# A hybrid encoder layer (axial attention beside a bidirectional mLSTM, then SwiGLU): the opening with squares summed on TensorE and four projection tiles in the first batch

## The chip, the cores and the metric

The kernel runs on one core of a Trainium2 chip. A core has five engines that work side by side, each through its own list of instructions in order: TensorE (PE in the profile; PEld is its weight load) multiplies matrices into PSUM, VectorE (DVE), ScalarE (ACT) and GpSimd (POOL) work on rows of elements, SyncE (SP) issues most transfers. The metric is the device time of one execution, in microseconds (us), the median of several runs.

## The reference

One layer over a sequence of 1024 positions with 1024 features, batch 1, all in float32:

```python
cond = jax.nn.silu(c)
mod = cond @ w_ada[l] + b_ada[l]
sh1, sc1, g1, sh2, sc2, g2 = jnp.split(mod, 6, axis=-1)
h = modulate(rms_norm(x, norm_mix_g[l]), sh1, sc1)      # h*(1+scale) + shift
proj = h @ w_in[l]
q_a, k_a, v_a, qk_m, v_m, o_m, gates = jnp.split(proj, splits, axis=-1)
y_attn = axial_gqa_attention(q_a, k_a, v_a, q_norm_g[l], k_norm_g[l], tables)
y_mem = bidirectional_mlstm(qk_m, v_m, o_m, gates, conv_w[l], conv_b[l], gate_b[l], mlstm_norm_g[l])
mix = jnp.concatenate([y_attn, y_mem], axis=-1) @ w_out[l]
x = x + g1[:, None, :] * mix
h = modulate(rms_norm(x, norm_ffn_g[l]), sh2, sc2)
x = x + g2[:, None, :] * ((jax.nn.silu(h @ w_gate[l]) * (h @ w_up[l])) @ w_down[l])
return rms_norm(x, final_norm_g)
```

The attention has 8 query heads and 2 key heads of 64 features, with a norm and a rotation of q and k; the mLSTM has 4 heads of 128 and runs over chunks of 64 positions in both directions.

## The kernel before

Everything is held transposed: features on the 128 partitions, the 1024 positions along the row. x comes as eight tiles of 128 features (k = 0 to 7); a row is worked on in two halves of 512 positions (n = 0, 1).

**Products in three parts.** A float32 factor is split into a high part, rounded to the fast format fp32r, and the low rest. A product of w and h is then three matmuls into the same sum (`mm3`, L295 to L297): whi x hh, whi x hl, wlo x hh. So each h (tile k, half n) needs ScalarE for `hh` (a copy) and an element-wise engine for `hl` (x - hh: VectorE for k = 0, POOL for the others), and each weight piece ScalarE for `whi` and POOL for `wlo`. A piece is 128 x 512: four k of one tile of 128 output features. Pieces sit in a ring of six; `load_piece` asks for the next one, and its transfer goes through `wst`, a ring of three. In the trace the matmuls of the first batch appear as `acc<-hh,whi`, `acc<-hl,whi`, `acc<-hh,wlo`; those that produce positions on the partitions (for v, o and the gates of the mLSTM) as `acct`.

**The opening.** ScalarE squares each half of a tile of x (`sq<-x`), VectorE and POOL add the squares up (`ssx<-ssx,sq`), and one matmul with ones per half sums over the partitions (`ms<-ssx,ones`, L549). `rstd_steps` makes 1/sqrt from it: a ScalarE estimate, then one Newton step on VectorE (the `sq<-ms`, `sq<-sq` rows). Warm-up matmuls (`acc<-con,ones`) run before and after these sums (WARM0, L547, and WARM, L555); their results are overwritten.

**Modulation.** The row c comes replicated over the partitions as `cond`. For each 128 features of the shift (j = 0 to 7) and of the scale (j = 8 to 15) `ada_load(j)` loads 128 x 1024 weights and multiplies them by `cond` with a running sum (`ada<-ada,cond` on VectorE; j = 0 has its product on POOL and its sum on ScalarE). `h_steps(k)` then adds the biases in columns of 128x1 (`mod<-modacc,vec`), forms the factor (`sc<-mod,vec`), multiplies the tile by rstd on VectorE (`x<-x,sq`), applies factor and shift on ScalarE (`x<-x,mod,sc`), and splits the result.

**The first batch.** For k = 0 to 7 TensorE adds up three projection tiles in PSUM: attention's k, v and q0 (`acc0[0]` to `acc0[2]`). Behind it a stream of units, in the order of `IN`, does the rest of the projection; K and q are rotated by `rope_steps`, v is turned by `v_steps`. At the same time `gate_steps`, a chain of short operations on VectorE and ScalarE with small transposes on TensorE (T, from L819 to L918), prepares the mLSTM's gates. The attention starts with its first score matmul (S, L974) when q's rotation and the gates are done; the rest of the projection fills TensorE's gaps in it. Then comes the mLSTM (`ni<-Cs,mq` is one of its matmuls), with the output projection as filler, then the feed-forward part.

**What sets the order.** The program is written out by a planner, the class `Clock`. Each step is emitted with an expected duration; steps that are ready run in the order of expected times, and `need` holds TensorE's next instruction back until what it needs has been emitted. So the order of each engine's list follows from the costs in the code, such as `ck.pe(0.65)` for three matmuls. Such a list is then fixed: an engine that waits for one instruction lets none of the later ones past.

Of the kernel before, what the change touches and what calls it, by code (L numbers as in the profile page):

```python
# [11 lines left out]
F32 = mybir.dt.float32  # L12
# [28 lines left out]
WARM = 6  # L41
WARM0 = 9
POOLED = (0,)
# [4 lines left out]
IN = ([("t", 0), ("q", 1), ("q", 2), ("q", 3), ("f", 0), ("f", 4), ("f", 1), ("f", 5), ("t", 2), ("f", 2), ("f", 6),  # L48
# [21 lines left out]
class Flag:  # L70
    """done: what sets it is emitted; t: when that is expected to end"""
# [12 lines left out]
class Engine:  # L84
    """An engine's instructions with their expected times."""
# [39 lines left out]
class Clock:  # L125
    """Emits instructions in the order of expected times (us), each engine's in the order in which they are ready."""
# [16 lines left out]
    def chain(self, delay, *steps, flag=None, bg=None):  # L143
        """Functions that follow one another. bg: the engine of each step; the step waits until that is idle."""
# [35 lines left out]
    def need(self, *flags):  # L180
        """What sets the flags is emitted before what follows."""
# [14 lines left out]
    def add_pe(self, dt):  # L196
        """work of the tensor engine that is not a stream's"""
        self.t += dt
# [6 lines left out]
    def streams(self, mains, fills=(), stop=None):  # L205
        """Runs streams, the first that is ready first, until the mains have ended or stop() holds."""
# [14 lines left out]
class Stream:  # L221
    """A part of the tensor engine's work: a generator that yields the flags that its next piece needs."""
# [15 lines left out]
def layer_kernel(ctx, tc, xT, c, w_ada, vecs, cons, rope, w_f, w_t0, w_t, w_o, w_gu, w_d, out):  # L238
# [8 lines left out]
    # ---------------------------------------------------------------- constants  # L247
    both = const.tile([P, 2], F32, name="both")
# [22 lines left out]
    # DRAM scratch  # L271
# [39 lines left out]
    def psum_open(name, tags, bufs=1):  # L311
        """tags: name -> (tag, buffers)"""
# [7 lines left out]
    class slot:  # L320
        """what frees the next tile of a tag"""
# [26 lines left out]
    with tc.manual_schedule():  # L348
# [12 lines left out]
        def load_cond(pool):  # L361
            """silu of c, the same for all partitions"""
# [11 lines left out]
        # ---------------------------------------------------- weights in a ring of six pieces  # L374
# [33 lines left out]
        specs = conv_w(0) + conv_w(1) + conv_w(2)  # L408
# [12 lines left out]
        def raw(shape, src, flag, arrived):  # L421
            """a transfer into the ring of three; flag: it has been used; arrived(tile, delay)"""
# [10 lines left out]
        def split(p, delay, src, shape, *before, lo=None):  # L433
            """the parts of a piece"""
# [12 lines left out]
        def piece(i):  # L447
            """a piece; its transfer, where it has one of its own"""
# [11 lines left out]
        def load_piece():  # L460
            """the next piece, once there is room for it"""
# [17 lines left out]
        # ---------------------------------------------------- norm 1, modulation, first three tiles  # L479
# [11 lines left out]
        ssx = [stp.tile([P, HALF], F32, tag="ssx", name="ssx", bufs=2) for _ in range(NH)]  # L491
        sq_ok = {}
        for k in range(KT):
            def sum_up(k=k):
# [1566 lines left out]
```

## Time and profile before

| | us |
|---|---|
| median of 3 runs (1430.2 to 1435.06) | 1433.75 |
| span of the profiled execution | 1431.8 |
| TensorE busy in it | 1310.1 |
| VectorE busy | 1075.9 |
| POOL busy | 792.6 |
| ScalarE busy | 660.6 |
| TensorE's first instruction (warm-up) | 7.59 |
| first batch done, first `acct` matmul | 89.76 |
| first score of the attention | 206.75 |

A time-line row gives start, duration, engine, line, operation, out<-in, shapes and count, and in brackets how long the engine had been idle and what released it. A row of groups gives line, engine, operation, names and shapes, count, then busy time and the mean in ns, then the idle time ahead. L96 is a helper through which all operations of VectorE, ScalarE and POOL pass, so these are told apart by their names.

### The profile page before, as it was taken

Reading aid. Unit: us, or ns where it says so; the run is one execution under the profiler, and the core shown is the slowest. Engines: PE = TensorE matmul, PEld = TensorE weight load, DVE = VectorE, ACT = ScalarE, POOL = GpSimd, SP = SyncE. Lnnn points to the kernel's source line nnn. Section 1 sums busy time; section 2 is a strip of 40 time slices with the busy share of each in tenths; the row PEclk is TensorE's granted clock in tenths of the full one; section 3 lists DMA queues with packets and bytes.
Section 4 is the critical chain, followed back from the end, with each engine's and each line's share of the span. In section 5 each row is a group of like instructions: output and inputs, shape, how many; then the busy total and the mean of one; then the engine's idle time right before and its main releaser. Section 6 shows DMA issues by size and latency. Waiting matters only on the chain.

```text
span 1431.8 us, 19550 instructions
## 1 busy us (share of the span) xinstructions
PE 1310.1 (91%) x6594; PEld 1075.7 (75%) x6602; DVE 1075.9 (75%) x1542; ACT 660.6 (46%) x1191; POOL 792.6 (55%) x624
## 2 busy tenths in 40 slices
PE   5789799999999999899877899999999999979997
PEld 2577677888878988777655688888888887757786
DVE  6947989987788836776899786766666654988676
ACT  5444326677666645454555333332333234433462
POOL 5555454444444336766557564554544444799942
PEclk9899899999999999999999999999999999999999
DMA  7446452322112144824742342232333159623324
GB/s 285 158 127 198 148 153 78 118 66 77 44 52 60 38 136 127 291 94 165 239 155 67 102 141 103 96 106 101 111 110 102 62 185 339 247 67 88 103 63 151
DMA packets 103172, 184.40 MB, mean 129 GB/s; under 512 B 11296, under 2 KB 32672, under 8 KB 103072
## 3 DMA queue, kind: packets, MB, share of 16 engines
q1 hardware_dynamic: 89968, 161.06, 35.2%
q10 hardware_dynamic: 13104, 22.10, 4.2%
q8 instruction: 52, 0.85, 0.3%
q14 instruction: 48, 0.39, 0.1%
HBM read 136.19 MB, written 43.25 MB: 125 GB/s over the span
## 4 chain that ended last, share of the span: by engine, by line
PE 55%; DVE 19%; issue 8%; DMA 7%; POOL 6%; ACT 3%; SPq 1%; DVEq 0%; POOLq 0%; ACTq 0%
PE acc L296 13%; PE acc L295 13%; PE acc L297 13%; POOL wlo L96 3%; DVE x L96 3%; DVE ada L96 3%; DVE sst L96 3%; PE av L1025 2%; DMA wst<-act_d 2%; PE T L1006 2%; DVE PT L96 2%; PE S L974 2%; DVE y L96 2%; PE acct L295 2%; PE acct L297 1%
## 5 line engine op out<-in xcount | busy, mean ns | idle before, releaser
L96 POOL TENSOR_TENSOR wlo<-wst,whi 128x512 fp32r<-128x512 f32 (+2 forms) x208 | 309.0, 1492 | 227.4 <-ACT whi L96 211.2
L96 ACT ACTIVATE whi<-wst 128x512 fp32r<-128x512 f32 (+2 forms) x219 | 131.9, 606 | 141.8 <-PE acc L297 22.4
L96 POOL TENSOR_SCALAR P<-P,sst 128x1024 f32<-128x1024 f32 x64 | 88.9, 1392 | 141.2 <-DVE sst L96 99.8
L296 PE MATMUL acc<-x,whi 128*128 128x512 f32 x352 | 139.6, 397 | 3.3 <-DVE x L96 3.3
L96 POOL TENSOR_TENSOR wlo<-wr,whi 128x512 fp32r<-128x512 f32 x60 | 83.5, 1392 | 78.3 <-ACT whi L96 74.9
L295 PE MATMUL acc<-hh,whi 128*128 128x512 f32 x224 | 97.8, 436 | 13.5 <-ACT hh L96 11.3
L297 PE MATMUL acc<-whi,wcl 128*128 128x512 f32 x244 | 98.1, 402 | 9.5 <-POOL wcl L96 9.5
L96 ACT ACTIVATE P<-S,sst,colq 128x1024 f32<-128x1024 f32 x64 | 77.3, 1207 | 52.2 <-DVE sst L96 47.8
L295 PE MATMUL acc<-whi,wch 128*128 128x512 f32 x244 | 96.8, 397 | 4.0 <-ACT wch L96 4.0
L296 PE MATMUL acc<-hl,whi 128*128 128x512 f32 x224 | 92.8, 414 | 8.2 <-POOL hl L96 4.5
L296 PE MATMUL acc<-wlo,wch 128*128 128x512 f32 x244 | 96.9, 397 | 1.1 <-POOL wlo L96 1.1
L297 PE MATMUL acc<-hh,wlo 128*128 128x512 f32 x224 | 91.5, 409 | 0.0
L96 DVE SCALAR_TENSOR_TENSOR ada<-ada,cond 128x512 f32<-128x512 f32 (+1 forms) x79 | 84.9, 1082 | 7.3 <-DMA ada<-in_w_ada_dram 7.2
L96 DVE TENSOR_TENSOR sg<-acc,sg 128x512 f32<-128x512 f32 x67 | 45.4, 687 | 59.3 <-PE acc L297 58.9
L96 ACT ACTIVATE PT<-T 128x512 fp32r<-128x512 f32 x128 | 71.4, 597 | 37.8 <-PE T L1006 37.1
L96 DVE TENSOR_TENSOR PT<-T,PT 128x512 fp32r<-128x512 f32 x128 | 82.8, 681 | 7.2 <-ACT PT L96 7.1
L96 ACT ACTIVATE whi<-wr 128x512 fp32r<-128x512 f32 x60 | 37.9, 632 | 106.1 <-DVE wr L96 49.6
L96 POOL TENSOR_TENSOR wlo<-s,whi 128x512 fp32r<-128x512 f32 x44 | 60.8, 1383 | 38.3 <-ACT whi L96 31.7
L295 PE MATMUL acct<-whi,hh 128*128 128x256 f32 (+1 forms) x256 | 79.3, 310 | 2.4 <-ACT xp L96 1.0
L296 PEld LDWEIGHTS acc<-x,whi 128*128 128x128 f32 x352 | 66.5, 189 | 19.2 <-DVE x L96 4.2
L96 DVE SCALAR_TENSOR_TENSOR x<-acc,mod,x 128x512 f32<-128x512 f32 (+1 forms) x92 | 62.7, 719 | 24.1 <-PE acc L297 24.1
L1006 PE MATMUL T<-con,P 128*128 128x128 f32 x512 | 70.2, 275 | 10.4 <-DVE PT L96 7.6
(457 smaller groups left out, 3875.1 us busy)
## 6 DMA issues: line engine op xcount, KB each, us to landing
wr<-in_w_gu_dram SPq DMA_DIRECT2D x66, 256.0 KB, 2.8
ada<-in_w_ada_dram SPq DMA_DIRECT2D x64, 256.0 KB, 3.6
wd<-in_w_d_dram SPq DMA_DIRECT2D x22, 512.0 KB, 7.0
wst<-in_w_gu_dram SPq DMA_DIRECT2D x34, 256.0 KB, 3.1
wst<-act_d SPq DMA_DIRECT2D x33, 256.0 KB, 4.1
ada<-in_w_ada_dram SPq DMA_DIRECT2D x16, 512.0 KB, 4.9
wst<-in_w_o_dram SPq DMA_DIRECT2D x32, 256.0 KB, 4.3
act_d<-sg ACTq DMA_DIRECT2D x31, 256.0 KB, 2.0
```

What stands on the lines that cost most here:

```text
L96: return fn(*args, **kw)
L295: nc.tensor.matmul(acc, w[0], x[0], start=first, stop=False)
L296: nc.tensor.matmul(acc, w[0], x[1], start=False, stop=False)
L297: nc.tensor.matmul(acc, w[1], x[0], start=False, stop=last)
L974: nc.tensor.matmul(sp[:, halves(n)], qs[:, j * P:(j + 1) * P], k2[g][m][:, halves(n)], start=m == 0, stop=m == 1)
L1006: nc.tensor.transpose(tp[:, k], Pt[q][:, (4 * b + k) * P:(4 * b + k + 1) * P], ident)
L1025: nc.tensor.matmul(av, va[:, k, h // 4], PT[it][m][:, k], start=(k, m) == (0, 0), stop=(k, m) == (NJ - 1, 1))
```

## The change

- The squares are no longer added up by VectorE and POOL. Each of the 16 half tiles goes to TensorE, which sums them in PSUM (16 matmuls `ms<-sq,ones`, L519 of the new program). Squares have a ring of six instead of four, and those of tile k wait for the sums of tile k - 3. The first warm-up is 6 matmuls instead of 9, the second 4 instead of 6.
- The first batch has four tiles: k, v, q0 and q1. q1 leaves the units of `IN`. For k = 7 the batch goes tile by tile instead of half by half.
- The first eight weight pieces come by half: k 0 to 3 of all four tiles, then k 4 to 7. Three are asked for at the start, three after the sums of squares, the last two when k = 3 is done.
- `ada` 0 is made on VectorE like the others, and no `ada` waits for rstd.
- Of modulation's column work the shift goes to ScalarE (one operation with a bias); for the factor b_ada + 1 is formed once for all tiles, and one VectorE operation takes the place of two adds and the factor's own operation.
- ScalarE does one small operation early for the table of the square root.
- K is rotated ahead of V's turning; q1's rotation follows K's.

```diff
-WARM = 6
-WARM0 = 9
-POOLED = (0,)
+WARM = 4
+WARM0 = 6
+NT0 = 4
-IN = ([("t", 0), ("q", 1), ("q", 2), ("q", 3), ("f", 0), ...
+IN = ([("t", 0), ("q", 2), ("q", 3), ("f", 0), ...
...
-        specs = conv_w(0) + conv_w(1) + conv_w(2)
+        specs = [conv_w(f)[b] for b in range(2) for f in range(NT0)]
...
-            return stp.tile([P, HALF], F32, tag="sq", name="sq", bufs=4)
+            return stp.tile([P, HALF], F32, tag="sq", name="sq", bufs=6)
         load_cond(bp)
         ck.table = "silu"
+        act.activation(both[:, 2:3], eps, AF.Abs_reciprocal_sqrt)
...
-                for n in range(NH):
-                    sq = ssx[n] if k == 0 else small()
-                    act.activation(sq, x_t[k][:, halves(n)], AF.Square)
-                    if k:
-                        (gps if n and k < 6 else dve).tensor_add(ssx[n], ssx[n], sq)
-            sq_ok[k] = ck.chain(dma(x_t[k], xT[k]), sum_up)
+                sq_t[k] = [small() for _ in range(NH)]
+                for n in range(NH):
+                    act.activation(sq_t[k][n], x_t[k][:, halves(n)], AF.Square)
+            sq_ok[k] = ck.chain(dma(x_t[k], xT[k]), *([summed_ok[k - 3]] if k > 2 else []), squares)
...
-            if j in POOLED:
-                steps = [lambda: gps.tensor_mul(t, t, PP["cond"]),
-                         lambda: act.activation(t, t, AF.Copy, accum_out=modacc[:, 0, j:j + 1])]
-            else:
-                steps = [lambda: dve.scalar_tensor_tensor(t, t, 1.0, PP["cond"], ...)]
-            ada_at[j] = ck.chain(dma(t, w_ada[j]), *([] if j in (0, 8) else [rstd_done]), *steps)
+            ada_at[j] = ck.chain(dma(t, w_ada[j]), lambda: dve.scalar_tensor_tensor(
+                t, t, 1.0, PP["cond"], op0=OP.mult, op1=OP.mult, accum_out=modacc[:, 0, j:j + 1]))
         for j in (8, 0):
             ada_load(j)
-        load_piece()
-        load_piece()
-        ck.need(sq_ok[4])
-        load_piece()
-        load_piece()
-        for j in (9, 1):
-            ada_load(j)
-        ck.need(sq_ok[7])
-        load_piece()
-        load_piece()
+        for _ in range(3):
+            load_piece()
+        acc0 = [[psum_any([P, HALF], "acc") for _ in range(NH)] for _ in range(NT0 - 1)]
+        for _ in range(WARM0):
+            nc.tensor.matmul(acc0[0][0], ones, con[:, 0:HALF], start=True, stop=True)
+        for k in range(KT):
+            ck.need(sq_ok[k])
+            for n in range(NH):
+                nc.tensor.matmul(msp[n], ones, sq_t[k][n], start=k == 0, stop=k == KT - 1)
+                ck.pe(0.86)
+            summed_ok[k].set(ck, ck.t)
+            if k == 4:
+                for j in (9, 1):
+                    ada_load(j)
+        for _ in range(3):
+            load_piece()
...
-        for _ in range(WARM0):
-            nc.tensor.matmul(acc0[0][0], ones, con[:, 0:HALF], start=True, stop=True)
         for n in range(NH):
-            nc.tensor.matmul(msp[n], ones, ssx[n], start=True, stop=True)
-            ck.pe(0.86)
             rstd_ok.append(rstd_steps(msp[n], 1.0 / D, f"n{n}", ...))
-        ck.chain(0.0, *rstd_ok, *[lambda: None] * 2, flag=rstd_done)
+        b1 = stp.tile([P, KT], F32, name="b1")
+        dve.tensor_scalar(b1, V("b_ada", 8, KT), 1.0, None, op0=OP.add)
...
-                dve.tensor_add(mod[:, k:k + 1], modacc[:, 0, k:k + 1], V("b_ada", k))
-                dve.tensor_add(mod[:, 8 + k:9 + k], modacc[:, 0, 8 + k:9 + k], V("b_ada", 8 + k))
-                dve.scalar_tensor_tensor(sc1[:, k:k + 1], mod[:, 8 + k:9 + k], 1.0, V("norm_mix_g", k), ...)
+                act.activation(mod[:, k:k + 1], modacc[:, 0, k:k + 1], AF.Identity, bias=V("b_ada", k))
+                dve.scalar_tensor_tensor(sc1[:, k:k + 1], modacc[:, 0, 8 + k:9 + k], b1[:, k:k + 1],
+                                         V("norm_mix_g", k), op0=OP.add, op1=OP.mult)
...
+        ck.need(*rstd_ok)
+        acc0.append([psum_any([P, HALF], "acc") for _ in range(NH)])
         for k in range(KT):
-            for n in range(NH):
-                while k not in h_ok:
-                    ck.pop()
+            while k not in h_ok:
+                ck.pop()
+            for n, f in ([(n, f) for n in range(NH) for f in range(NT0)] if k < KT - 1 else
+                         [(n, f) for f in range(NT0) for n in range(NH)]):
                 ck.need(h_ok[k][n])
-                for f in range(3):
-                    mm3(acc0[f][n], weights(2 * f, k, 4), (h_hi[k][:, halves(n)], h_lo[k][:, halves(n)]),
-                        k == 0, k == KT - 1)
-                    ck.pe(0.65)
-                    if n == 1 and k % 4 == 3:
-                        load_piece()
+                mm3(acc0[f][n], weights(NT0 * (k // 4) + f, k % 4, 4), (...), k == 0, k == KT - 1)
+                ck.pe(0.69)
+                if n == 1 and k % 4 == 3:
+                    load_piece()
...
-        v_steps([(a, Flag()) for a in acc0[1]])
         rope_steps(4, [(a, Flag()) for a in acc0[0]])
+        v_steps([(a, Flag()) for a in acc0[1]])
         ck.at(2.5, lambda: rope_steps(0, [(a, Flag()) for a in acc0[2]]))
+        ck.chain(0.0, *k2_ok, lambda: rope_steps(1, [(a, Flag()) for a in acc0[3]]))
```

How this moves instructions is seen in the lists of the engines. In these lists hh_215 to hh_222 and hl_223 to hl_230 are the parts of h for k = 0 to 7; the tiles of x are x_239 to x_246 before and x_240 to x_247 now.

TensorE's first instructions, before:

```order
L547 MATMUL acc<-con,ones 128x512 x9
L549 MATMUL ms<-ssx,ones 128x512 x2
L555 MATMUL acc<-con,ones 128x512 x6
L295 MATMUL acc<-hh_215,whi 128x512
L296 MATMUL acc<-hl_223,whi 128x512
```

and now:

```order
L515 MATMUL acc<-con,ones 128x512 x6
L519 MATMUL ms<-sq,ones 128x512 x16
L550 MATMUL acc<-con,ones 128x512 x4
L295 MATMUL acc<-hh_215,whi 128x512
L296 MATMUL acc<-hl_223,whi 128x512
```

The sums over x are 16 matmuls behind a shorter warm-up, where they were two behind a longer one.

POOL from its first work on x to the end of the first batch, before:

```order
L96 TENSOR_TENSOR ssx<-ssx,sq 128x512 x5
L96 TENSOR_TENSOR ada<-ada,cond 128x1024
L96 TENSOR_TENSOR wlo<-wst,whi 128x512 x5
L96 TENSOR_TENSOR hl_224<-x_240,hh_216 128x512
L96 TENSOR_TENSOR wlo<-wst,whi 128x512
...
L96 TENSOR_TENSOR hl_228<-x_244,hh_220 128x512 x2
L96 TENSOR_TENSOR wlo<-wst,whi 128x544 x2
L96 TENSOR_TENSOR hl_229<-x_245,hh_221 128x512
L96 TENSOR_TENSOR wlo<-wst,whi 128x544
L96 TENSOR_TENSOR hl_229<-x_245,hh_221 128x512
L96 TENSOR_TENSOR hl_230<-x_246,hh_222 128x512 x2
```

and now:

```order
L96 TENSOR_TENSOR wlo<-wst,whi 128x512 x6
L96 TENSOR_TENSOR hl_224<-x_241,hh_216 128x512 x2
...
L96 TENSOR_TENSOR hl_228<-x_245,hh_220 128x512 x2
L96 TENSOR_TENSOR hl_229<-x_246,hh_221 128x512 x2
L96 TENSOR_TENSOR hl_230<-x_247,hh_222 128x512 x2
L96 TENSOR_TENSOR wlo<-wst,whi 128x512 x2
L96 TENSOR_TENSOR wlo<-wst,whi 128x544 x2
```

The adds of squares and `ada` 0 are gone. Before, all six pieces of the batch were split ahead of the last `hl` of k = 1. Now six of eight are split ahead of every `hl` of POOL, and the last two, which the matmuls of k = 4 need for tiles q0 and q1, stand behind the `hl` of k = 7. On ScalarE the two `whi` stand likewise behind the `hh` of k = 7.

VectorE from the sums of squares to its first `hl`, before:

```order
L96 TENSOR_SCALAR sq<-ms 128x512 x2
L96 SCALAR_TENSOR_TENSOR sq<-sq,ms 128x512
L96 SCALAR_TENSOR_TENSOR sq<-sq 128x512
L96 SCALAR_TENSOR_TENSOR sq<-sq,ms 128x512
L96 SCALAR_TENSOR_TENSOR sq<-sq 128x512
L96 TENSOR_TENSOR mod<-modacc,vec 128x1 x2
L96 SCALAR_TENSOR_TENSOR sc_343<-mod,vec 128x1
L96 TENSOR_TENSOR x_239<-x_239,sq 128x512
L96 SCALAR_TENSOR_TENSOR ada,modacc<-ada,cond 128x1024 x2
L96 TENSOR_TENSOR x_239<-x_239,sq 128x512
L96 TENSOR_TENSOR hl_223<-x_239,hh_215 128x512
```

and now, from the last step of the square root on:

```order
L96 SCALAR_TENSOR_TENSOR sq<-sq 128x512 x2
L96 SCALAR_TENSOR_TENSOR ada,modacc<-ada,cond 128x1024
L96 TENSOR_TENSOR x_241<-x_241,sq 128x512
L96 TENSOR_TENSOR x_240<-x_240,sq 128x512 x2
L96 TENSOR_TENSOR x_241<-x_241,sq 128x512
L96 SCALAR_TENSOR_TENSOR sc_349<-modacc,b_350,vec 128x1
L96 TENSOR_TENSOR x_242<-x_242,sq 128x512
L96 SCALAR_TENSOR_TENSOR ada,modacc<-ada,cond 128x1024 x2
L96 TENSOR_TENSOR x_242<-x_242,sq 128x512
L96 TENSOR_TENSOR hl_223<-x_240,hh_215 128x512
```

The first `hl` stands behind products of three tiles of x instead of one, and `ada` products stand between the steps of the square root.

More of the change, by code (lines that the diff above doesn't have):

```diff
@@ L47 @@
 NP = NF // 2
[L48 removed]
+IN = ([("t", 0), ("q", 2), ("q", 3), ("f", 0), ("f", 4), ("f", 1), ("f", 5), ("t", 2), ("f", 2), ("f", 6),
        ("f", 3), ("f", 7), ("t", 1), ("t", 3)])
@@ L245, in layer_kernel @@
     mid = midpool.__enter__()
-    both = const.tile([P, 2], F32, name="both")
+    both = const.tile([P, 3], F32, name="both")
     mhalf, eps = both[:, 0:1], both[:, 1:2]
@@ L484, in small, with squares @@
         def small():
[L485 removed]
+            return stp.tile([P, HALF], F32, tag="sq", name="sq", bufs=6)
         load_cond(bp)
         ck.table = "silu"
+        act.activation(both[:, 2:3], eps, AF.Abs_reciprocal_sqrt)
         x_t = [stp.tile([P, S], F32, tag="x", name=f"x{k}", bufs=KT) for k in range(KT)]
         msp = [psum_any([P, HALF], "ms") for _ in range(NH)]
[L491 to L492 removed]
+        sq_ok, sq_t = {}, {}
+        summed_ok = [Flag() for _ in range(KT)]
         for k in range(KT):
[L494 removed]
+            def squares(k=k):
+                sq_t[k] = [small() for _ in range(NH)]
                 for n in range(NH):
[L497 to L502 removed]
+                    act.activation(sq_t[k][n], x_t[k][:, halves(n)], AF.Square)
+            sq_ok[k] = ck.chain(dma(x_t[k], xT[k]), *([summed_ok[k - 3]] if k > 2 else []), squares)
         ada_at = {}
```

9 lines of the change are left out of this document (3 added, 6 removed).

## The prediction

> **What bounds the kernel now.** I read the page first, then the time line of the opening engine by engine, then busy times by stage.
>
> ```profile
> span 1431.8 us, 19550 instructions
> PE 1310.1 (91%) x6594; PEld 1075.7 (75%) x6602; DVE 1075.9 (75%) x1542; ACT 660.6 (46%) x1191; POOL 792.6 (55%) x624
> 24.50:77.20 52.70, 35.08 (x120) 23.59 (x119) 51.34 (x75) 27.51 (x42) 31.39 (x20) 0.86 0.49 159
> 118.80:176.60 57.80, 47.37 (x210) 37.88 (x209) 49.26 (x73) 25.12 (x35) 34.10 (x20) 0.90 0.55 174
> 176.60:206.70 30.10, 28.59 (x111) 23.02 (x112) 22.03 (x29) 6.49 (x10) 14.00 (x10) 0.85 0.58 172
> 206.70:506.70 300.00, 285.02 (x1872) 249.81 (x1871) 254.86 (x428) 196.54 (x342) 134.02 (x99) 1.00 0.23 67
> 506.70:650.20 143.50, 133.09 (x826) 117.05 (x833) 93.32 (x221) 73.87 (x201) 90.89 (x135) 0.99 0.51 167
> ```
>
> The span is 1.95 under the median 1433.75; the sum is made against the span and added to the median. TensorE is busy 91% overall, but in the modulation (24.5 to 77.2) VectorE is the bound: 51.34 of 52.70, TensorE 35.08. (A row of this view: stretch, its length, then busy time and instructions of TensorE, its weight loads, VectorE, ScalarE and POOL; granted clock, share of the DMA engines, GB/s.) The next rows are the gate chain, its last step to the first score, the attention and the mLSTM stage; in the attention stage TensorE has 285.02 of 300.
>
> ```profile
> 7.59 9.95 PE L547 MATMUL acc<-con,ones 128*128 128x512 f32 x18 [7.59 <-DMA con<-in_cons_dram]
> 11.80 3.60 PE L547 MATMUL acc<-con,ones 128*128 128x512 f32 x8
> 12.65 1.02 PE L547 MATMUL acc<-con,ones 128*128 128x512 f32 x2
> 22.37 2.08 PE L549 MATMUL ms<-ssx,ones 128*128 128x512 f32 x2 [1.62 <-DVE ssx L96]
> 41.35 0.79 PE L296 MATMUL acc<-hl,whi 128*128 128x512 f32 x1 [3.73 <-DVE hl L96]
> 57.84 0.50 PE L296 MATMUL acc<-hl,whi 128*128 128x512 f32 x1 [1.39 <-POOL hl L96]
> 78.62 0.79 PE L295 MATMUL acc<-hh,whi 128*128 128x512 f32 x1 [4.56 <-ACT hh L96]
> 82.28 0.63 PE L295 MATMUL acc<-hh,whi 128*128 128x512 f32 x1
> 82.71 0.63 PE L296 MATMUL acc<-hl,whi 128*128 128x512 f32 x1
> 89.76 0.29 PE L295 MATMUL acct<-whi,hh 128*128 128x272 f32 x1
> 118.85 0.60 PE L819 MATMUL T<-con,gI 128*128 128x128 f32 x4
> 170.26 0.39 PE L295 MATMUL acc<-hh,whi 128*128 128x512 f32 x1
> 172.13 0.40 PE L297 MATMUL acc<-hh,wlo 128*128 128x512 f32 x1
> 176.62 0.66 PE L918 MATMUL T<-dexp,ones 64*128 64x64 f32 x2 [4.09 <-DVE dexp L96]
> 206.75 2.01 PE L974 MATMUL S<-k,qs 128*128 128x512 f32 x8
> ```
>
> TensorE waits for VectorE's products from 22 to 82, ends the first batch at 89.76, and then waits again for the gate chain until 176.62. An fp32 matmul shows as two rows (nine warm-ups, 18 rows); the groups of 8 and of 2 give 3.60 - 1.02 = six pitches of 0.43.
>
> **The change, term by term.**
>
> *Squares on TensorE.* The rows above put the start at 7.59 (the constants). Six warm-ups end at 7.59 + 9.95 - 6 x 0.43 = 14.96; sixteen fp32 sums, 32 rows x 0.43 = 13.8, end at 28.7, where the second sum ended at 22.37 + 2.08 = 24.45. They are late by 4.3, and replace adds of VectorE and POOL that lay beside the transfers of x. The data don't set this: at 22.37 all squares had even been added up, and TensorE reaches the last tile at 27.0.
>
> *The VectorE chain.* Before, the last product of a tile of x ends at 74.85 + 2.35 = 77.20, 52.75 after the sums:
>
> ```profile
> 30.63 0.69 DVE L96 TENSOR_TENSOR x<-x,sq 128x512 f32<-128x512 f32 x1
> 31.23 1.22 DVE L96 SCALAR_TENSOR_TENSOR ada<-ada,cond 128x1024 f32<-128x1024 f32 x1
> 32.37 1.22 DVE L96 SCALAR_TENSOR_TENSOR ada<-ada,cond 128x1024 f32<-128x1024 f32 x1
> 45.66 0.22 DVE L96 TENSOR_TENSOR mod<-modacc,vec 128x1 f32<-128x1 f32 x2
> 45.92 0.16 DVE L96 SCALAR_TENSOR_TENSOR sc<-mod,vec 128x1 f32<-128x1 f32 x1
> 48.34 1.32 DVE L96 TENSOR_TENSOR mod<-modacc,vec 128x1 f32<-128x1 f32 x2
> 48.28 1.30 POOL L96 TENSOR_TENSOR hl<-x,hh 128x512 fp32r<-128x512 f32 x1 [3.63 <-ACT hh L96]
> 74.85 2.35 DVE L96 TENSOR_TENSOR x<-x,sq 128x512 f32<-128x512 f32 x2
> L96 DVE TENSOR_TENSOR mod<-modacc,vec 128x1 f32<-128x1 f32 x16 | 8.3, 557 | 0.0
> L96 POOL TENSOR_TENSOR wlo<-wst,whi 128x512 fp32r<-128x512 f32 x6 | 9.9, 1662 | 6.4 <-ACT whi L96 6.3
> L96 POOL TENSOR_TENSOR wlo<-wst,whi 128x544 fp32r<-128x544 f32 x3 | 4.6, 1535 | 2.4 <-ACT whi L96 2.4
> ```
>
> The pair of column adds takes 0.22 with POOL idle and 1.32 where a POOL subtraction of 1.30 starts at the same time: the two engines take turns, and most of the 8.3 is waiting for POOL, which the next VectorE instruction would inherit. So the merge is worth 8 x (45.92 - 45.66) = 2.1, not 8.3. The same 14 `ada` products, 16 of x and two `hl` remain behind the sums, and their order changes. POOL loses from this stretch six of nine weight splits: three go ahead of the sums, the three of 544 columns behind the last `hl`. Alone, a POOL row costs VectorE about 1.25. VectorE's own pitches come to 14 x 1.14 (`ada`, start to start) + 18 x 0.60 (x and `hl`) + 8 x 0.34 (columns) + 5 x 0.6 (the root of the mean square) = 32.5 of the 52.7; the other 20 over 20 POOL rows of 1.25 is a share of about 0.8, so six give 6. The chain ends at 28.7 + 52.75 - 2.1 = 79.4 less 0 to 7.5, by the share at 73.4; splits that leave let an `hl` start earlier and collide in their place, so I give some back: 75.0.
>
> *Four tiles, weights by half.* The last two pieces of the second half (tiles q0 and q1 of k 4 to 7) now stand on ScalarE behind the last `hh` and on POOL behind the last `hl`. TensorE does 96 matmuls of k 0 to 3 and 6 of k = 4, then waits. Before, all six pieces were split ahead, and 82.40 - 77.20 = 5.2 passed from the last product to the last of three POOL rows; now the same count, two `hl` and a `wlo`, stands there:
>
> ```profile
> 78.65 3.75 POOL L96 TENSOR_TENSOR hl<-x,hh 128x512 fp32r<-128x512 f32 x3 [0.25 <-ACT hh L96]
> ```
>
> TensorE resumes at 75.0 + 5.2 = 80.2, 0.5 more for the second piece. It has 90 of 192 matmuls left, where before only those of the last tile of h were. At (172.13 - 170.26) / 8 = 0.234 each (seven rows lie between) they take 21.1; with eight at the half clock's 0.43, as after the wait of 4.56, 22.6. Taking the middle, the batch ends at 102.5: 12.7 later. Tile q1's 48 matmuls, 11.2, no longer follow. Net +1.5.
>
> The clock: after 1.39 idle at 57.84 the row is 0.50, after 4.56 idle at 78.62 rows stay 0.43 apart until 83. The Trainium skill ("TensorE: Matmul & The Clock Gate", "Part 1: The HAM clock gate (the "warmup" mystery)") halves the clock after an idle window of about 3.4 us, whose phase floats; the two rows agree. By it two waits under 3.4 each would cost nothing, and the sum would be 0.7 lower.
>
> *The gate chain starts later.* It runs on VectorE and ScalarE, 57.8 from 118.85 to 176.62 with TensorE busy only 47.37. Started 12.7 later it ends near 189.4. Then 30.1 passed to the first score, 28.59 of it TensorE work, of which 57 `acc` matmuls (13.4) are gone, being q1's or done in the gate stage. The first score comes between 189.4 + 16.7 = 206.1, if TensorE alone is the bound, and 219.5, if the dependent steps are: 0 to 13 of extra wait. Middle: +6.
>
> *The fill work is dealt out anew.* Counted in the order, between the first score and the last `av` stand 87 more `acct` matmuls (312 to 399) and six more `acc`; up to the last `ni` in the mLSTM stage 87 `acct` fewer. At 0.118 for 256 columns, from the rows here, 87 are 10.3, and TensorE is the bound in attention:
>
> ```profile
> 117.90 0.28 PE L296 MATMUL acct<-wlo,hh 128*128 128x272 f32 x1
> 118.02 0.29 PE L297 MATMUL acct<-whi,hl 128*128 128x272 f32 x1
> L1787 PE MATMUL ni<-Cs,mq 128*128 128x260 f32 x62 | 19.7, 400 | 7.7 <-DVE num L96 7.3
> ```
>
> (0.12 for 272 columns.) The mLSTM stage gives them back only while TensorE bounds it; its `ni` waits 7.3 for VectorE, and 10.4 of its 143.5 are idle. Between 0 and 10.3 are lost; I take the middle, +5.2. The six `acc` change sides of the first score only.
>
> *Costed at nothing.* One more table load and a column operation on ScalarE, hidden in its wait for `cond`; the shift column on ScalarE, hidden by its waits for x; `ada` 0 on VectorE, hidden because VectorE has lost its adds before 28.7. Were that cover gone they would cost about 1.3, 0.6 and 1.2. K's rotation ahead of V's is covered by the 80 us and more to the first score. On the SP queue a third weight piece goes ahead of `ada` 9 and 1: 0.26 MB, 1.6 at the 159 GB/s of the first window above, hidden because VectorE first uses them after 28.7.
>
> ```profile
> 1.64 1.28 ACT L96 ACT_TABLE_LOAD   x1 [1.64 <-PEq L2049]
> 5.37 1.06 ACT L96 ACTIVATE cond<-cond 128x1024 f32<-128x1024 f32 x1 [2.45 <-DMA cond<-in_c_dram]
> ACT x L96 <- DVE x L96: 24.9, 14, 5.4
> ```
>
> Sum: 1.5 + 6 + 5.2 = +12.7, so 1433.75 + 12.7 = 1446.4.
>
> **Rivals.**
> *The later stages absorb it* (0.08): the gate chain's lateness is filled and the mLSTM stage gives all back. Then +1.5, 1435.3, no measurable change. For it: in 176.6 to 206.7 TensorE is busy 28.59 of 30.10. Against: TensorE waits 4.09 for the chain at 176.62 already.
> *TensorE never stops at k = 4* (0.05, the other side): the last pieces are split before TensorE needs them. Its first `hl` waits behind two more `ada` pairs and six more products of x, so it starts some 7.6 later than 41.35, at 49.0; twelve matmuls at 0.43 and 180 at 0.234 end at 96.3, 6.5 later than 89.76, less 11.2: -4.7. With the rest absorbed, 1429. It decides where the second `wlo` is done before TensorE gets there, 49.0 + 5.2 + 90 x 0.234 = 75.3. Against: it stands behind `hl` of the last tile, which can't start before 75.
> *Both later terms in full* (0.10): 1.5 + 13 + 10.3 = +24.8, 1458.5. For it: rows of the gate chain wait on each other, not on TensorE.
> *My forecast* has 0.77.
>
> **Numbers.** 0.3% (4.3 us) is about what this measurement can tell from no change; the runs before span 1430.2 to 1435.06. Slower: the forecast and the costly case, 0.87; same 0.08; faster 0.05. With one later term absent and the chain at 73.4 the sum is 12.7 - 5.2 or 6 - 1.6, some +5; halfway between that and nothing is 1437. With the gate term in full and the chain 3 later it is 12.7 + 7 + 3 = +22.7, 1456.4. Range 1437 to 1456, all but about 2 in 10.
>
> **What would show it.** In the profile after: sums end near 28.7; the first `hl` matmul near 49; a wait of TensorE for `whi` and `wlo` within k = 4 near 75 to 80; first `acct` near 102.5; the last gate matmul near 189; the first score near 213; the attention stage longer, the mLSTM stage shorter by less. The forecast is wrong if that wait is absent, if the first score comes by 207, or if POOL's turns hardly slow VectorE, in which case the chain ends far below 73.

## The result and the profile after

The changed kernel took 1452.97 us (median of 4, 1446.94 to 1455.7) where the kernel before took 1432.85 beside it: a ratio of 1.0122, 95% interval 1.0096 to 1.0148. Repeated later on one chip with the experiments it was 1452.31 against 1434.37, 1.0124 (1.0101 to 1.0148). A ratio as recorded can differ a little from the quotient of the two medians. It is slower by some 14 to 21, where 12.7 was forecast.

The profiled execution has a span of 1445.2, 13.4 over the one before. Its page:

```profile
span 1445.2 us, 19555 instructions
PE 1315.2 (91%) x6620; PEld 1080.8 (75%) x6620; DVE 1064.1 (74%) x1520; ACT 658.4 (46%) x1199; POOL 773.7 (54%) x618
```

VectorE and POOL have 11.8 and 18.9 less to do, TensorE 5.1 more, and the span grew. The time line of the opening says where, first on TensorE, then on the three engines that feed it at the end of the chain:

```profile
7.68 7.57 PE L515 MATMUL acc<-con,ones 128*128 128x512 f32 x12 [7.68 <-DMA con<-in_cons_dram]
15.08 13.90 PE L519 MATMUL ms<-sq,ones 128*128 128x512 f32 x32
49.31 0.80 PE L296 MATMUL acc<-hl,whi 128*128 128x512 f32 x1 [4.02 <-DVE hl L96]
78.95 0.50 PE L295 MATMUL acc<-hh,whi 128*128 128x512 f32 x1 [3.08 <-ACT whi L96]
79.29 0.40 PE L296 MATMUL acc<-hl,whi 128*128 128x512 f32 x1
81.72 0.79 PE L297 MATMUL acc<-hh,wlo 128*128 128x512 f32 x1 [2.02 <-POOL wlo L96]
86.15 0.63 PE L295 MATMUL acc<-hh,whi 128*128 128x512 f32 x1
86.57 0.63 PE L296 MATMUL acc<-hl,whi 128*128 128x512 f32 x1
87.31 0.39 PE L295 MATMUL acc<-hh,whi 128*128 128x512 f32 x1
104.68 0.29 PE L295 MATMUL acct<-whi,hh 128*128 128x272 f32 x1
199.42 0.40 PE L914 MATMUL T<-dexp,ones 64*128 64x64 f32 x2 [4.80 <-DVE dexp L96]
211.83 0.86 PE L970 MATMUL S<-k,qs 128*128 128x512 f32 x3
```

```profile
74.11 2.38 DVE L96 TENSOR_TENSOR x<-x,sq 128x512 f32<-128x512 f32 x2
78.29 1.68 ACT L96 ACTIVATE whi<-wst 128x512 fp32r<-128x512 f32 x3
77.94 2.50 POOL L96 TENSOR_TENSOR hl<-x,hh 128x512 fp32r<-128x512 f32 x2 [2.00 <-ACT hh L96]
80.39 3.80 POOL L96 TENSOR_TENSOR wlo<-wst,whi 128x512 fp32r<-128x512 f32 x3
```

The sums end at 15.08 + 13.90 = 28.98 (before 24.45). The last product of x ends at 76.49 (77.20), almost as before, but TensorE then stands in the middle of k = 4: `whi` of the late piece comes behind the last `hh`, `wlo` behind the last `hl`. It goes on at 81.72, for 5.4 us at half its clock (rows 0.43 apart until 87), and ends the batch at 104.68 instead of 89.76.

For the stages behind it, rows on one kind of matmul give first and last start; those of the kernel before first, then those of the changed one, its repetition last:

```profile
L1025 PE MATMUL av<-PT,va x512: 276/280/385, 225.6 to 506.7; 128*128 128x256 f32 x171
L1787 PE MATMUL ni<-Cs,mq x64: 380/382/613, 531.0 to 650.9; 128*128 128x260 f32 x64
```

```profile
L1021 PE MATMUL av<-PT,va x512: 276/281/386, 232.3 to 527.7; 128*128 128x256 f32 x171
L1783 PE MATMUL ni<-Cs,mq x64: 380/383/487, 550.7 to 665.8; 128*128 128x260 f32 x64
```

```profile
L1783 PE MATMUL ni<-Cs,mq x64: 380/383/487, 552.8 to 668.0; 128*128 128x260 f32 x64
```

| stage | before | after | difference |
|---|---|---|---|
| start to end of the first batch | 89.76 | 104.68 | +14.9 |
| to the first score | 116.99 | 107.15 | -9.8 |
| to the last `av` (attention) | 299.95 | 315.87 | +15.9 |
| to the last `ni` (mLSTM) | 144.2 | 138.1 | -6.1 |
| to the end of the span | 780.9 | 779.4 | -1.5 |

So at the first score the change is 5 behind, at the end of the attention 21. The repetition has a span of 1451.1: its last `ni` is at 668.0, 17.1 later than before, and the rest takes 783.1. The profile first shown is one of the shorter executions.

### The profile page after: what moved, and what is told of

Its sections match the earlier page's. It is cut to its first block, busy times and chain, and to the rows that moved or that the text cites. A ratio compares the mean times of both kernels' runs of the same rounds, so it can differ in the third digit from the quotient of the medians.

```text
span 1445.2 us, 19555 instructions
## 1 busy us (share of the span) xinstructions
PE 1315.2 (91%) x6620; PEld 1080.8 (75%) x6620; DVE 1064.1 (74%) x1520; ACT 658.4 (46%) x1199; POOL 773.7 (54%) x618
## 4 chain that ended last, share of the span: by engine, by line
PE 57%; DVE 23%; issue 7%; POOL 4%; DMA 4%; ACT 4%; SPq 1%; ACTq 0%; DVEq 0%; POOLq 0%
PE acc L296 14%; PE acc L295 14%; PE acc L297 14%; DVE x L96 4%; DVE ada L96 3%; PE av L1021 3%; DVE sst L96 2%; POOL wlo L96 2%; PE T L1002 2%; PE S L970 2%; DVE y L96 2%; DVE PT L96 2%; DMA ada<-in_w_ada_dram 1%; POOL wcl L96 1%; DVE s L96 1%
## 5 line engine op out<-in xcount | busy, mean ns | idle before, releaser
L96 POOL TENSOR_TENSOR wlo<-wst,whi 128x512 fp32r<-128x512 f32 (+2 forms) x208 | 302.4, 1460 | 244.5 <-ACT whi L96 230.8
L96 POOL TENSOR_SCALAR P<-P,sst 128x1024 f32<-128x1024 f32 x64 | 83.8, 1310 | 165.8 <-DVE sst L96 148.2
L96 DVE SCALAR_TENSOR_TENSOR ada<-ada,cond 128x512 f32<-128x512 f32 (+1 forms) x80 | 81.1, 1017 | 21.8 <-DMA ada<-in_w_ada_dram 12.4
L96 DVE TENSOR_REDUCE sst<-S 128x1 f32<-128x1024 f32 x64 | 77.8, 1215 | 6.1 <-PE S L970 5.8
L1002 PE MATMUL T<-con,P 128*128 128x128 f32 x512 | 71.2, 276 | 12.2 <-DVE PT L96 10.3
```

The lines of the kernel that those rows point to most:

```text
L96: return fn(*args, **kw)
L1002: nc.tensor.transpose(tp[:, k], Pt[q][:, (4 * b + k) * P:(4 * b + k + 1) * P], ident)
```

## The experiments

All are timed against the kernel before on the same chip. "Batch" is the first `acct` matmul, "rest" the span less that.

| run | median | ratio, 95% interval | batch | rest |
|---|---|---|---|---|
| before | 1432.9 to 1434.4 | 1 | 89.76 | 1342.0 |
| changed | 1452.97 | 1.0122 (1.0096 to 1.0148) | 104.68 | 1340.5 |
| e5, changed again | 1452.31 | 1.0124 (1.0101 to 1.0148) | 103.9 | 1347.2 |
| e1, adds back | 1444.24 | 1.0066 (1.0047 to 1.0085) | 97.24 | 1344.7 |
| e2, no stop in k = 4 | 1438.89 | 1.0041 (1.0023 to 1.0059) | 96.11 | 1340.8 |
| e3, three tiles | 1432.84 | 0.9995 (0.9981 to 1.0009) | 87.00 | 1346.9 |
| e4, columns only | 1429.14 | 0.9965 (0.9950 to 0.9980) | 85.55 | 1341.8 |
| e6, squares only | 1437.34 | 1.0006 (0.9989 to 1.0024) | 93.24 | 1344.4 |
| e7, no first warm-up | 1446.01 | 1.0081 (1.0057 to 1.0104) | 98.42 | 1345.6 |
| e8, three tiles, no first warm-up | 1428.99 | 0.9966 (0.9950 to 0.9982) | 84.25 | 1343.0 |
| e9, the same with fp32r sums | 1428.25 | 0.9959 (0.9941 to 0.9976) | 81.03 | 1345.1 |
| e10, fill capped | 1461.42 | 1.0182 (1.0163 to 1.0201) | 104.4 | 1357.7 |
| e11, three tiles, adds back | 1423.93 | 0.9920 (0.9904 to 0.9936) | 79.71 | 1343.1 |
| e12, four tiles, both faults mended | 1431.67 | 0.9980 (0.9964 to 0.9995) | 88.75 | 1342.2 |

**e1: the squares back on VectorE and POOL.**

```diff
...
-            def squares(k=k):
-                sq_t[k] = [small() for _ in range(NH)]
+            def sum_up(k=k):
+                ...
                 for n in range(NH):
-                    act.activation(sq_t[k][n], x_t[k][:, halves(n)], AF.Square)
+                    sq = ssx[n] if k == 0 else small()
+                    act.activation(sq, x_t[k][:, halves(n)], AF.Square)
+                    if k:
+                        (gps if n and k < 6 else dve).tensor_add(ssx[n], ssx[n], sq)
...
```

> The changed kernel with one part undone: the squares are added up on VectorE and POOL as before, with two sums on TensorE and the old warm-ups (9 and 6); four tiles, weights by half and the merged column work stay. Theory A (lateness in the opening is carried to the end): the sums end near 24.5 instead of 28.8, the last product of x near 72, TensorE's wait in k = 4 stays but ends some 4 to 7 earlier, the first batch ends near 98 to 100 instead of 104.7, the first score 4 to 7 earlier than 211.8, and the time is 4 to 7 under the changed kernel's, some 1446 to 1449. Theory B (what costs is the fill work dealt anew in the attention, and earlier stages are absorbed): the attention keeps its 399 acct matmuls, so the time stays within 3 of the changed kernel's 1453.

```profile
19.81 1.98 PE L524 MATMUL ms<-ssx,ones 128*128 128x512 f32 x4 [1.08 <-DVE ssx L96]
72.46 0.80 PE L295 MATMUL acc<-hh,whi 128*128 128x512 f32 x1 [4.43 <-ACT whi L96]
75.20 0.79 PE L297 MATMUL acc<-hh,wlo 128*128 128x512 f32 x1 [1.51 <-POOL wlo L96]
97.24 0.29 PE L295 MATMUL acct<-whi,hh 128*128 128x272 f32 x1
```

The sums end at 21.8, 7.2 earlier, and the batch 7.4 earlier; the medians differ by 8.1 to 8.7. The lateness is carried to the end, as A has it; the waits in k = 4 stay. That the sums end even before those of the kernel before is because `ada` 0 is no longer on POOL beside the adds: seven of VectorE's adds took 10.42 there, and one of them, beside that product, 2.83; with `ada` 0 on VectorE behind them the seven took 8.28 in e1 and 8.30 in e11, whose row is the last.

```profile
11.89 10.42 DVE L96 TENSOR_TENSOR ssx<-ssx,sq 128x512 f32<-128x512 f32 x7 [0.25 <-ACT sq L96]
19.49 2.83 DVE L96 TENSOR_TENSOR ssx<-ssx,sq 128x512 f32<-128x512 f32 x1
18.89 2.88 POOL L96 TENSOR_TENSOR ada<-ada,cond 128x1024 f32<-128x1024 f32 x1 [1.08 <-DMA ada<-in_w_ada_dram]
```

```profile
12.00 8.30 DVE L96 TENSOR_TENSOR ssx<-ssx,sq 128x512 f32<-128x512 f32 x7 [0.23 <-ACT sq L96]
```

**e2: tiles k and v first from k = 4 on.**

```diff
-        for k in range(KT):
-            ...
-            for n, f in ([(n, f) for n in range(NH) for f in range(NT0)] if k < KT - 1 else
-                         [(n, f) for f in range(NT0) for n in range(NH)]):
+        late = [(k, n, f) for k in range(4, KT) for f in (2, 3) for n in range(NH)]
+        for k, n, f in [(k, n, f) for k in range(KT) for n in range(NH) for f in range(NT0) if k < 4 or f < 2] + late:
```

> The changed kernel with TensorE's order in the first batch altered: from k = 4 on tiles k and v come first for all k, and q0 and q1 (whose pieces are split last) behind them; nothing else is edited. Theory A: no wait in k = 4; when the last product of x is there, 60 matmuls are left instead of 90, so the batch ends 30 x 0.234 = 7 earlier, near 98, and the time is 5 to 10 under the changed kernel's, 1443 to 1448. The planner will deal the fill work otherwise as well (336 acct between first score and last av in its list, not 399), so the attention should be some 63 x 0.118 = 7 shorter and the mLSTM stage as much longer. Theory B: the batch ends 7 earlier, but the time falls only by what the attention's fill returns and the mLSTM stage doesn't take, under 3.

No wait of TensorE is left between 55 and the end of the batch at 96.11, 8.6 earlier, and the median is 13.4 to 14.1 lower than the changed kernel's: the stop costs most of the loss. It is more than the 7 of the matmuls, since the half clock goes as well (granted 1.00 from 74 to 96; its sums also end 0.5 earlier). The attention takes 306.9 (first score 201.7, last `av` 508.6), 9 less than in the changed kernel, where 7 was expected; but the mLSTM stage takes 151.3 (last `ni` 659.9), 13 more, so what is gained is what the batch gains. Still e2 is slower than the kernel before, though its first score is 5 earlier.

**e3: three tiles.** NT0 = 3, and `("q", 1)` is back in `IN`.

> The changed kernel with three tiles in the first batch: q1 is a unit of the stream again; weights by half with six pieces in the ring of six, squares on TensorE and merged column work stay. Theory A: every piece is split before it is needed, no wait in k = 4; the late sums (+4.3) and the merged column work with fewer splits between (-2 to -8) about cancel, so the batch ends within 3 of 89.8 and the fill is as before (312 acct in the attention): the time is that of the kernel before within 5, 1430 to 1438. If the cost were in the squares on TensorE rather than in the fourth tile, it would keep most of the loss, 1443 and more.

Level with the kernel before, and the whole loss of 1.2% is gone: without the fourth tile the squares on TensorE and the rest of the change cancel.

**e4: the column work alone,** on the kernel before.

```diff
-                dve.tensor_add(mod[:, k:k + 1], modacc[:, 0, k:k + 1], V("b_ada", k))
-                dve.tensor_add(mod[:, 8 + k:9 + k], modacc[:, 0, 8 + k:9 + k], V("b_ada", 8 + k))
-                dve.scalar_tensor_tensor(sc1[:, k:k + 1], mod[:, 8 + k:9 + k], 1.0, V("norm_mix_g", k), ...)
+                act.activation(mod[:, k:k + 1], modacc[:, 0, k:k + 1], AF.Identity, bias=V("b_ada", k))
+                dve.scalar_tensor_tensor(sc1[:, k:k + 1], modacc[:, 0, 8 + k:9 + k], b1[:, k:k + 1], ...)
```

> The kernel before with one part of the change alone: the shift's column on ScalarE, the factor's column in one VectorE operation with b_ada + 1 made once. If VectorE and POOL take turns, so that the long column rows were waits that the next instruction inherits (the prediction's step): the chain is 2.1 shorter, the batch ends near 87.7, the time 0 to 2 lower. If the rows' own 8.3 were their cost: the batch ends near 82 and the time is some 5 to 8 lower, 1425 to 1428.

The stretch from the end of the sums (24.62) to the last product of x (74.53), then TensorE's last wait in the batch and the rows where its pitch changes behind it:

```profile
24.60:74.50 49.90, 37.62 (x122) 25.39 (x120) 48.74 (x59) 29.20 (x51) 31.40 (x19) 0.86 0.48 159
75.71 0.50 PE L296 MATMUL acc<-hl,whi 128*128 128x512 f32 x1 [3.35 <-POOL hl L96]
76.52 0.63 PE L296 MATMUL acc<-hl,whi 128*128 128x512 f32 x1
79.93 0.39 PE L295 MATMUL acc<-hh,whi 128*128 128x512 f32 x1
85.55 0.29 PE L295 MATMUL acct<-whi,hh 128*128 128x272 f32 x1
```

The chain is 2.8 shorter (49.9 for 52.7): near the 2.1 of turn-taking, far from 8.3. The batch ends 4.2 earlier. Of this, 2.9 is that TensorE goes on at 75.71 instead of 78.62; the rest is a second wait of 0.56 that is gone, one row done ahead of the wait, and some 0.5 from the clock, since the first three rows still run at its full pitch. The clock falls all the same: from 76.52 to 79.93 the rows stand 0.43 apart. The median is 5.1 lower (2.9 to 7.2 by the interval). So the part is worth more than the 0 to 2 expected, and mostly because TensorE starts again earlier.

**e5: the changed kernel again.**

> The changed kernel once more, unedited, so that it stands beside the next three on one chip; its first four runs spread from 1446.9 to 1455.7. By the sum of stages (first score +5, attention +16, mLSTM stage -6, rest -1.5) the ratio to before is 1.009 to 1.010. If the first median stands, it is 1.012 to 1.014.

The first median stands.

**e6: squares alone,** on the kernel before (three tiles, pieces tile by tile).

> The kernel before with one part of the change alone: the 16 squares go to TensorE, six warm-ups ahead of them, ring of six; three tiles, the pieces tile by tile, ada 0 on POOL and the column work as before. Theory A: the sums end near 28.7 instead of 24.45, everything behind them is 4 later, the batch ends near 93 to 94 and the time is 3 to 5 higher, 1437 to 1439. Theory B (the chain behind the sums takes it back, since POOL and VectorE are free earlier): the batch ends within 1.5 of 89.8 and the time is that of before.

In its profile the sums end at 29.6, the batch 3.5 later, the span is 5.8 longer. Of the times this can't be said: the median is 3 higher, the interval from 0.9989 to 1.0024 allows none. Between A and B it stays open in time, and is A's in the profile.

**e7: the changed kernel without its first warm-ups** (WARM0 = 0).

> The changed kernel without the six warm-ups ahead of the sums of squares. Theory A (TensorE, not the data, sets the end of the sums): they start near 8 and end some 3 to 5 earlier than 28.8, at 24 to 26, though the first rows run at the half clock; the batch and the first score come 3 to 5 earlier, and the time is 3 to 6 under the changed kernel's. If the squares or the transfers of x set it, the sums end near 28.7 as now and nothing changes. If the warm clock is what the warm-ups buy, the sums end later than now and the time rises by 1 to 4.

```profile
8.23 15.47 PE L519 MATMUL ms<-sq,ones 128*128 128x512 f32 x32 [8.23 <-ACT sq L96]
98.42 0.29 PE L295 MATMUL acct<-whi,hh 128*128 128x272 f32 x1
```

The sums end at 23.7, 5.3 earlier, at the price of 1.6 for cold first rows; the batch is 6.3 and the time 6.3 to 7 lower. TensorE set the end of the sums.

**e8: three tiles without the first warm-ups.**

> Three tiles in the first batch, pieces by half, squares on TensorE, merged column work, and no warm-ups ahead of the sums: a version that may beat both. Theory A: the run with three tiles and six warm-ups ended its batch at 87.0 and was level with the kernel before; sums 3 to 5 earlier bring the batch to 82 to 84 and the time to 3 to 6 under before, 1428 to 1431. Theory B (the lateness in the opening is absorbed later): level with before, 1432 to 1436.

1428.99, as A has it: 0.3% under the kernel before.

**e9: e8 with the squares and ones in fp32r.**

```diff
-                sq_t[k] = [small() for _ in range(NH)]
+                sq_t[k] = [stp.tile([P, HALF], F32R, tag="sq", name="sq", bufs=6) for _ in range(NH)]
-                nc.tensor.matmul(msp[n], ones, sq_t[k][n], start=k == 0, stop=k == KT - 1)
+                nc.tensor.matmul(msp[n], onesr, sq_t[k][n], start=k == 0, stop=k == KT - 1)
```

> The run with three tiles and no first warm-ups, with one more edit: the squares are written as fp32r and summed with ones in fp32r, so that each sum is one pass over 512 columns at the pitch of the kernel's other fp32r matmuls (0.234) instead of two of 0.43. Theory A (the sums' end sets the chain and the chain sets the rest): the sums end with the data at 18 to 19 instead of 25.2, the last product of x ends some 5 to 6 earlier than 72.7, the batch ends at 78 to 80 instead of 84.2, and the time is 4 to 6 lower than with fp32 sums, 1423 to 1425. Rival (the chain then waits for ada weights, which land at about one in 1.3 us behind x, or for the weight splits): the batch gains less than 3.

```profile
8.08 10.42 PE L521 MATMUL ms<-sq,onesr 128*128 128x512 f32 x16 [8.08 <-ACT sq L96]
69.18 2.44 DVE L96 TENSOR_TENSOR x<-x,sq 128x512 f32<-128x512 f32 x2
18.50:71.60 53.10, 37.00 (x119) 25.48 (x119) 52.51 (x65) 28.85 (x50) 34.02 (x20) 0.84 0.53 179
81.03 0.29 PE L295 MATMUL acct<-whi,hh 128*128 128x272 f32 x1
```

The window row runs from the end of the sums to the last product of x. The same stretch of e8:

```profile
25.20:72.70 47.50, 29.90 (x104) 21.65 (x103) 47.33 (x59) 24.92 (x42) 26.50 (x15) 0.75 0.45 145
```

The sums end at 18.5, 6.7 earlier than e8's 25.2, but the last product of x ends at 71.6, and the batch is 3.2 earlier; the time is the same. A is wrong here: the chain from the sums to the last x grew from 47.5 to 53.1. Of the expectation's two rivals for it, late `ada` weights are not the cause: VectorE is busy 52.51 of the 53.10 and doesn't wait for them. POOL works 34.0 in the chain instead of 26.5, its first three splits now behind the sums, and one `ada` product more (1.14) stands there: that leaves the splits, as far as these rows show.

**e10: less fill in the attention.** The projection's stream may run 200 of its pieces there.

> The changed kernel with the fill work capped in the attention: of the projection's stream only 200 pieces may run between the first score and the end of the attention, in the planner's list 270 acct matmuls instead of 399 (the kernel before: 312), the rest behind it. Theory A (the count of fill matmuls makes the attention longer): the attention is 129 x 0.13 = 16 shorter than 315.9, near 299, and the mLSTM stage as much longer or less: the time is 0 to 8 lower. Rival (with less fill the attention falls back on a floor of its own, the softmax chain on ScalarE, VectorE and POOL, since the fill that is left runs first and the end of the attention has none): it stays within 4 of 316 and the time is 4 to 8 higher, the work put off coming on top.

```profile
212.00:528.00 316.00, 289.04 (x1820) 250.40 (x1818) 258.55 (x437) 194.88 (x340) 126.65 (x101) 0.97 0.23 68
L1021 PE MATMUL av<-PT,va x512: 276/281/579, 232.1 to 530.2; 128*128 128x256 f32 x171
```

TensorE does 10 to 11 less in the stretch, and the attention is no shorter: first score 211.7, last `av` 530.2. From 495 on TensorE waits 8.0 in it for VectorE's `PT`. The work put off is paid behind it, 8.5 to 9 in the median. So the count of fill matmuls doesn't by itself set the length of the attention: once the fill has run out, TensorE waits for the attention's own steps.

**e11: three tiles with the adds back,** that is e3 with e1's edit.

> Three tiles with pieces by half, merged column work, ada products not held back behind the root, and the squares added up on VectorE and POOL as before: the change without its squares and its fourth tile, and a second version that may beat both. Theory A: the sums end at 23 to 24.5, the batch ends at 80 to 83, earlier than the 85.5 of the run with the column work alone, since the splits come ahead of the chain; the time is that much lower, 1424 to 1428. Rival: the order of the pieces is worth nothing, 1429.

```profile
19.75 1.98 PE L524 MATMUL ms<-ssx,ones 128*128 128x512 f32 x4 [2.32 <-DVE ssx L96]
79.71 0.29 PE L295 MATMUL acct<-whi,hh 128*128 128x272 f32 x1
```

The fastest: 1423.93, a ratio of 0.9920. It keeps the merged columns, `ada` 0 on VectorE and the pieces by half, and leaves out the squares on TensorE and the fourth tile.

**e12: four tiles, both faults mended,** e1 with e2's order.

> Four tiles in the first batch with both faults of the opening mended: the squares are added up on VectorE and POOL as before, and from k = 4 on tiles k and v come first. Against the run with three tiles and the adds back (1423.9) only the fourth tile is different. Theory A, amended by the runs so far (from the end of the batch to the end every kernel takes 1340 to 1347, whether q1 is done or not): the batch ends near 88 to 89, the first score comes near 194, some 4 before that run's 198.7, and still the time is 1429 to 1434, some 6 to 9 over that run, because the attention and the mLSTM stage grow by what q1 saved. If the loss lay in the late sums and in the stop alone, the fourth tile would cost nothing and the time would be 1422 to 1426.

e11's last rows of attention and mLSTM, then e12's:

```profile
L1022 PE MATMUL av<-PT,va x512: 276/280/386, 218.2 to 499.7; 128*128 128x256 f32 x171
L1784 PE MATMUL ni<-Cs,mq x64: 380/382/548, 523.6 to 643.2; 128*128 128x260 f32 x64
```

```profile
L1022 PE MATMUL av<-PT,va x512: 275/281/391, 217.0 to 502.3; 128*128 128x256 f32 x171
L1784 PE MATMUL ni<-Cs,mq x64: 380/383/773, 524.8 to 652.9; 128*128 128x260 f32 x64
```

The batch ends 9.0 later than e11's. The first score comes at 194.7 against 198.7, 4.0 earlier: up to there q1's work does come back (106.0 from batch to score, for 119.0). Then the attention takes 6.6 longer (307.6 for 301.0) and the mLSTM stage 7.1 (150.6 for 143.5), the rest 1.6 less, and the median is 7.7 higher. So the fourth tile, with the order that goes with it, costs by itself, and it loses after the first score. A part of the `acct` fill in the attention and the mLSTM stage's `ni`, grouped by line, again e11 and then e12:

```profile
L295 PE MATMUL acct<-whi,hh 128*128 128x256 f32 x104 | 32.4, 312 | 1.6 <-ACT xp L96 1.2 <-ACT vstg L96 0.5
L1784 PE MATMUL ni<-Cs,mq 128*128 128x260 f32 x64 | 20.2, 397 | 7.6 <-DVE num L96 7.3
```

```profile
L295 PE MATMUL acct<-whi,hh 128*128 128x256 f32 x112 | 34.3, 306 | 0.9 <-ACT vstg L96 0.5 <-ACT xp L96 0.4
L1784 PE MATMUL ni<-Cs,mq 128*128 128x260 f32 x64 | 21.7, 423 | 8.1 <-DVE num L96 7.4
```

Each of the three lines of a product has eight more `acct` in the attention; in the mLSTM stage a `ni` takes 423 ns for 397.

## Why the prediction was right, and where it was not

**The sums:** 28.7 forecast, 28.98 measured; e7 shows that TensorE set it.

**The chain on VectorE:** 49.0 forecast for the first `hl`, 49.31 measured; 75.0 for the last x, 76.49. The merge was put at 2.1 and took 2.8 off the chain (e4). That a short column row mostly waited for POOL is borne out: rows of 8.3 went and 2.8 came back. Of the 5.2 by which the chain is shorter (47.5 for 52.75) that leaves some 2.4 for the splits and the order, where 4.4 was forecast.

**The stop in k = 4:** forecast at 80.2 and 0.5 more, measured as waits of 3.08 and 2.02 that end at 81.72. e2 shows its price.

**The clock there:** I took the middle of full and half clock for the 90 matmuls, 21.8; the 88 of them behind the second wait took 22.96, with the half clock for 5.4. The Trainium skill's rule ("TensorE: Matmul & The Clock Gate", Part 1, an idle window of about 3.4 us), as I applied it to each wait by itself, would have kept the full clock. The trace disagrees: the granted clock fell at about 80.3, within the second of two waits of 3.08 and 2.02. Nor does it take two: single waits of 3.35 (e4), 2.67 (e6) and 2.00 (e9) were followed by the half clock too, 0.8, 0.6 and 1.5 after they had ended.

**The first score:** 213 forecast, 211.8 measured (214.0 in e5). That it came so near is luck, since its two parts were off and cancelled: the gate chain began at 135.2 and took 64.2, where 131.5 and 57.8 were assumed, so it ended at 199.4, not 189.4; and the rest to the first score took 12.4, less than the 16.7 that I had as the lower end.

**The fill:** the attention was to grow by 11.7 (10.3 and 1.4) and grew by 15.9, with TensorE busy 14.8 longer in it. The mLSTM stage gave 6.1 back, near half of 10.3, and the rest 1.5, in the repetition less than nothing. e10 shows that fewer fill matmuls need not make the attention shorter.

**Tile q1's 48 matmuls and the two later terms.** By the table's last column, in every kernel but the capped one 1340 to 1347 pass from the end of the batch to the end, whether q1 has been done by then or not. What the batch takes longer is lost in full: +14.9, and a span 13.4 to 19.3 longer. TensorE's busy time from the end of the batch to the end says how, before and after:

```profile
89.76:1431.80 1342.04, 1251.21 (x6417) 1038.48 (x6423) 1009.83 (x1446) 614.83 (x1122) 744.62 (x590) 0.98 0.39 124
```

```profile
104.68:1445.20 1340.52, 1240.41 (x6377) 1031.11 (x6375) 1012.77 (x1446) 607.92 (x1117) 732.05 (x588) 0.97 0.38 124
```

q1's work is gone, 10.8 less (forecast 11.2), but TensorE idles 100.1 instead of 90.8 there. Of these 9.3, 4.6 lie ahead of the first score, 1.1 in the attention, 0.4 in the mLSTM stage and 3.1 in the last stage. The forecast had such losses as its two later terms, +6 ahead of the first score and +5.2 behind it. So the idea holds, that work taken out turns into waits; but these terms were middles of 0 to 13 and 0 to 10.3, so that they came near is luck, and it put the second one on the fill of the attention and the mLSTM stage, where two thirds of it, 3.1 of 4.6, came in the last stage. In the repetition TensorE is 6.0 less busy and 11.2 more idle than before, in e12 7.5 less and 6.6 more than in e11.

The work that q1 no longer does between batch and first score lets other fill move forward (in e12 24 `acct` and nine `acc` more in the attention by its rows, some 5 of its 6.6). It lengthens the stages it moves into, and the last stage, though it has less left, isn't shorter by as much: in e12 TensorE works 5.9 less in it than in e11, and it is 1.6 shorter. Of the 7.1 that e12's mLSTM stage takes longer, 6.6 are TensorE's busy time: 21 more matmuls of the output projection and 24 fewer `acct`, some 2 together at the pitches above, and a granted clock of 0.97 for 0.99. Why the clock is lower there, and why the last stage waits more, stays open.

**The rivals:** "the later stages absorb it" and "TensorE never stops" fell with the first profile; "both later terms in full", 1458.5, lies above every run of the changed kernel.

## What to carry to other kernels

Idle time of an engine is room for moved work only if that work's inputs are ready within it: find where the last of them stands in each feeding engine's in-order list first. Here the added matmuls needed splits that stood last on ScalarE and POOL, so they ran behind the wait for VectorE, not in it. To see whether time saved early, or work done early, is kept, compare kernels by the time from one common landmark to the end, and split it into TensorE's busy and idle time.

## What the runs showed of the hardware

The granted clock fell to half behind waits of TensorE, and not always at once. Behind a wait of 4.56 us (before) TensorE went on at half. Behind single waits of 3.35 (e4), 2.67 (e6) and 2.00 (e9) the first rows kept the full pitch of 0.23; the rows 0.43 apart came 0.8, 0.6 and 1.5 us later and lasted some 3.4 us. Waits of 1.39 (before) and 1.43 (e9) had no such effect. In the changed kernel it fell within the second of waits of 3.08 and 2.02, and was back 5.4 us after that. Which moment decides is not shown.

VectorE is held up by POOL: an add of 128x512 beside a POOL product of 2.88 took 2.83, and 0.68 with POOL idle (e1).
